# Low parts of the weights taken off GpSimd in the first mixer and behind the second, and the residual's squares summed by products alone

## The chip, the cores and the metric

The program runs on one core of one Trainium2 chip. Its time is the device time of one execution in microseconds (us). The core has five engines that work side by side and wait for each other through semaphores: TensorE (PE in the rows; PEld is its weight load) multiplies matrices, VectorE (DVE) and ScalarE (ACT) work element by element, GpSimd (POOL) does so too, and SyncE (SP) starts the transfers from memory. What a matmul gives lands in PSUM, the other tiles lie in SBUF.

## The reference

The input is one sequence of 256 tokens of width 1024, all in float32. Two blocks follow each other. The first has a hybrid mixer (a gated part and a pooled part), a SwiGLU layer, an RWKV time mix and another SwiGLU layer; the second has a mixer of convolution and attention, and then a layer with a squared ReLU. What the change touches is this:

```python
# first block, layer 0: z = rms_norm(h) @ ab_w_in, then
y_a = gmlp_spatial_gate(za[..., :512], za[..., 512:], ...)   # u * (w_s @ rms_norm(v) + b)
y_b = multiscale_pool(z[..., 1024:], pool_w, pool_scale)     # windows 2, 4, 8, 16
h = h + concat([y_a, y_b]) @ ab_w_out
# second block, behind its token mixer (whose last product is with w_out)
x = x + gate1 * rms_norm_2(y, g_post_mix)
h = rms_norm_2(x, g_pre_mlp) * (1.0 + scale2) + shift2
y = square(relu(h @ w_mlp_in)) @ w_mlp_out                   # 1024 -> 4096 -> 1024
x = x + gate2 * rms_norm_2(y, g_post_mlp)
```

## The kernel before

The residual `h` lies in SBUF with channels on the partitions: 8 tiles of 128 channels by 256 tokens. All weights stream in as 2604 blocks of 128x128, eight to a chunk of 512 KB, in the order in which the program uses them.

**Products in three parts.** Each float32 weight chunk `raw` is cut into a high part `hi` (ScalarE, line 185) and the rest `lo = raw - hi` (line 186), and each activation into `xh` and `xl`. A block's product is then three matmuls: hi with xh, hi with xl, lo with xh. `take` hands out blocks in order and has the chunks cut 16 blocks ahead. Four buffers hold `hi` and four hold `lo`, so a chunk's `hi` waits until TensorE has left the chunk four places before it.

**Who makes the low part.** `Weights.share` decides. It is added up chunk by chunk, and where the sum reaches 1 the low part goes to GpSimd instead of VectorE. It is 1 in three stretches: in the first mixer from line 686 to line 746, in the second mixer from line 1545 to line 1720, and from line 1803 in `post` to line 1854 in `mlp`. It also says where `rsqrt` and the sums of squares are worked out.

**First mixer** (`mixer`). One loop over the 8 tiles of `h` makes the pooled part and `v`. Then come the products for `u` (32 blocks, `ps<-xh,hi` and so on), and in the midst of them four products `plps` of the pooled sums `pl` with `poolw`. The sums (`s`, `pl`) and the reciprocal root for `v` (`rs_t`, `rs_y`, `rs_p`) are VectorE's. `mixps` comes next, and then the products with `ab_w_out`.

**Behind the second mixer** (`post`, then `mlp`). `post` scales the mixer's result `pu` by a factor for each token, which lies broadcast in PSUM (`bcps`), and adds it to `h`, tile by tile. `after_h` then cuts each new tile into `xh` and `xl` (scaled by the column `gs`), squares two tiles an operation on ScalarE (`sq`), and adds the squares up (`Sums`). TensorE meanwhile runs the first 6 column blocks of `w_mlp_in` on this unnormalised input (`gemm_fold`: 6 blocks for each of the 8 tiles, 48 blocks, 144 matmuls called `fold`). Inside this loop the sum over the partitions (`sums`, a product with a column of ones), the reciprocal root and its broadcast (`bcps`, `bc`) are made; when it is done, `modulate` makes the normalised `xh`, `xl` (through `mod`) for the other 26 column blocks.

**Order on an engine.** Each engine works through its own list in order. The lists are made when the program is built, by a scheduler that may move an instruction past others of its engine, so the written order is not the final one.

Of the kernel before, what the change touches and what calls it, by code (L numbers as in the profile page):

```python
# [15 lines left out]
ALU = mybir.AluOpType  # L16
AX = mybir.AxisListType

P = 128
T = 256  # L20
D = 1024
# [6 lines left out]
EPS = 1e-6  # L28
# [110 lines left out]
class Weights:  # L139


    def __init__(self, nc, dram, raw_pool, hl_pool, look=16, ahead=2):
        self.nc, self.dram, self.rp, self.hp = nc, dram, raw_pool, hl_pool
        self.order = []
        self.raw, self.hl = {}, {}
        self.nload = self.nsplit = 0
        self.look, self.ahead = look, ahead
        self.hook = None

        self.share = self.acc = 0.0  # L150

        self.whole = set()
# [78 lines left out]
class Sums:  # L231

    def __init__(self, kern, urgent=False, gp=4):
        self.k, self.urgent, self.gp = kern, urgent, gp
        self.parts = []
        self.acc = None

    def part(self):  # L240
        t = self.k.mp.tile([P, 512], F32, tag="sq" if self.parts else "acc", name="sq", bufs=2)
        self.parts.append(t)
        return t
# [4 lines left out]

    def added(self):
        n = len(self.parts)  # L250
        if n > 1 and not (n == 4 and self.urgent):

            e = self.k.nc.gpsimd if not self.k.ws.share and n <= self.gp else self.k.nc.vector
            e.tensor_tensor(out=self.parts[0], in0=self.parts[0], in1=self.parts[-1], op=ALU.add)  # L254
        if n == 4 - self.urgent:
            self.k.tt(self.parts[0][:, 0:T], self.parts[0][:, 0:T], self.parts[0][:, T:2 * T], ALU.add)

    def done(self):
        assert len(self.parts) == 4
        return self.k.token_sums([self.parts[0][:, 0:T]] + self.parts[3:4] * self.urgent)  # L260


class Kern:
# [360 lines left out]
    def mixer(self, xs, sums, nxt):  # L624
# [3 lines left out]
        st = {}  # L628
# [52 lines left out]
        for k in range(KD):  # L681
# [1 line left out]
                self.mm3(psb[m // 2][:, (m % 2) * T:(m % 2 + 1) * T], self.ws.take([win(k, 8 + m)]), X(k),  # L683
                         k == 0 and m % 2 == 0, k == KD - 1)
            self.mm3_tok(psv, self.ws.take([win(k, 4 + i) for i in range(4)]), X(k), k == 0, k == KD - 1)
        self.ws.share = 1
        for i in range(2):
            epi_v(i, psv[i])
        m = self.tiny("vm", [P, 2], tag="n2m")
# [1089 lines left out]
    def post(self, X, ks, banks, gcol, xs, xcol, sums):  # L1779


        pss = {}
        sm = Sums(self, True)

        def epi(j, ps):
            pss[j] = ps
            sm.square(ps)

        self.gemm(X, ks, banks, epi)
        r = self.rstd(sm.done(), D, EPS, 2)  # L1790
        u = self.slot("pu")
        for m in range(KD):
            self.act(u[:, m, :], pss[m // 2][:, (m % 2) * T:(m % 2 + 1) * T], AF.Copy, scale=gcol[:, m:m + 1])

        self.gg = gg = self.slot("gg", (P, 2, 512))
        for i in range(2):
            ps = self.bank("gg")
            for k in range(4):
                dg = self.mid("dg", (P, P))
                self.ts(dg, self.cst("ident", 128), self.gs[:, 24 + 4 * i + k:25 + 4 * i + k], None, ALU.mult)  # L1800
                self.mm(ps[:, k * P:(k + 1) * P], self.cst("ones", 128), dg, k == 0, k == 3)
            self.act(gg[:, i, :], ps, AF.Copy)
        self.ws.share = 1
        self.busy(BUSY_POST)
        bc = self.bcast(r, psum=True)
        self.busy(BUSY_POST)
        for j in range(4):
            for m in (2 * j, 2 * j + 1):
                t = u[:, m, :]
                self.tt(t, t, bc, ALU.mult)  # L1810
                self.tt(self.h[:, m, :], self.h[:, m, :], t, ALU.add)
            self.after_h(j, xs, xcol, sums)

    def mlp(self, xs, sums):
        nc = self.nc
        flat = lambda ap: ap.rearrange("p a t -> p (a t)")
        st = {}
# [1 line left out]
        src = lambda m: (lambda k: full("w_mlp_in_2", 0, k, m * P))  # L1819

        def stats():
            st["r"] = self.rstd(sums.done(), D, EPS)

        def bc():
            st["bc"] = self.bcast(st["r"])
# [10 lines left out]
        for m, ps in enumerate(pss):  # L1836
            nc.vector.tensor_copy(out=bias[:, m:m + 1], in_=ps[:, T:T + 1])
            r = self.mid("rf", (P, T))
# [41 lines left out]
        def mean(src, i, tt, more):  # L1880
            m = self.tiny("fm", [P, 1], tag="fm")
            self.ts(m, src[:, tt, i:i + 1], 1.0 / D, more, ALU.mult, ALU.add)
            return m
# [25 lines left out]
        m = mean(ss, 1, 0, mean(ss, 0, 0, EPS))  # L1909
        gated(0, slice(512, D), pss[0])  # L1910
        finish(0, m, (slice(0, 512), slice(512, D)))
        m = mean(ss, 0, 1, EPS)
        for i in range(2):
# [4 lines left out]
            m = mean(ss, 1 + i, 1, m)  # L1918
# [4 lines left out]
    def run(self, stop=99):  # L1923
        nc, io = self.nc, self.io
        self.h = h = self.xp.tile([P, KD, T], F32, tag="h", name="h")
        self.pvt = self.cp.tile([P, NPV], F32, tag="pv", name="pvt")
        self.cstt = self.cp.tile([P, NCST], F32, tag="cst", name="cstt")
        nc.sync.dma_start(out=self.pvt[:, 0:8], in_=io["pv"][:, 0:8])
        self.warm()

        def load_x(k):
            nc.sync.dma_start(out=h[:, k, :], in_=io["x"][:, k, :])

        load_x(0)
        for _ in self.ws.load(2):
            pass
        for k in (1, 2):
            load_x(k)
            self.ws.load_to(k)
        for k in (3, 4, 5):  # L1940
            load_x(k)
        nc.sync.dma_start(out=self.cstt[:, 0:257], in_=io["cst"][:, 0:257])

        def simple(g):

            return lambda: (self.main_x(), self.pv(g, 0, 8), [(Sums(self, gp=4 if g[:3] == "ffn" else 1), None)])

        nx = simple("mix0")()
        with self.phase(11, 6):
            xs, gcol, sums = nx  # L1950

            def split_x(k):
                self.split_scaled(xs[0][:, k, :], xs[1][:, k, :], h[:, k, :], gcol[:, k:k + 1])

            split_x(0)
            for _ in self.ws.split(2):
                pass
            for k in (1, 2):
                split_x(k)
                for _ in self.ws.split(2):  # L1960
                    pass
            split_x(3)
            self.after(1, lambda: (load_x(6), load_x(7)))
            for k in range(4, KD):
                self.after(6 * k - 22, lambda k=k: split_x(k))
            for j in range(4):
                self.after(8 * j + 12, lambda j=j: self.after_h(j, None, None, sums))
            self.after(16, lambda: nc.sync.dma_start(out=self.cstt[:, 257:], in_=io["cst"][:, 257:]))
            self.after(28, lambda: nc.sync.dma_start(out=self.pvt[:, 8:], in_=io["pv"][:, 8:]))
            nx = self.mixer(nx[0], nx[2][0][0], simple("ffn0"))  # L1970
        self.dump("h0", h)
        if stop <= 0:
            return
        ada = self.pool("ada", 1, ctx0 := ExitStack())
        self.ap = ada
        steps = self.ada_setup()
        self.ws.plan_whole(24 * NF, 1)

        self.ws.plan_whole(24 * NF + 88, 18)
        self.bg = steps[:28]  # L1980
        self.bg_rate = 28 / 520.0
        with self.phase(6, 8):
            nx = self.ffn(0, nx[0], nx[2][0][0], lambda: (None, None, [(Sums(self, True), None)]))
        self.drain_bg()
        self.dump("h1", h)
        if stop <= 1:
            ctx0.close()
            return
        ctx0.close()
        with self.phase(8, 7):  # L1990
            nx = self.rwkv(nx[2][0][0], simple("ffn1"))
        self.dump("h2", h)
        if stop <= 2:
            return
        ada = self.pool("ada2", 1, ctx0 := ExitStack())
        self.ap = ada
        steps = self.ada_setup()
        self.bg = steps[28:]
        self.bg_rate = 20 / 330.0

        def to_mixer2():
            self.drain_bg()
            self.ada_done()
            xs = self.fold_x()
            self.fold_shift(xs, self.shift1)

            nc.sync.dma_start(out=self.cst("reset", T).bitcast(I32), in_=io["pos"].partition_broadcast(P))
            return xs, self.gs[:, 0:8], [(Sums(self, gp=3), None), (Sums(self, gp=3), self.pv("fin", 0, 8))]

        with self.phase(6, 8):  # L2010
            nx = self.ffn(1, nx[0], nx[2][0][0], to_mixer2)
        self.dump("mod", self.mod)
        ctx0.close()
        self.dump("h3", h)
        if stop <= 3:
            return

        def to_mlp():
            xs = self.fold_x()
            self.fold_shift(xs, self.shift2)  # L2020
            return xs, self.gs[:, 16:24], [(Sums(self), None)]

        with self.phase(13, 4):
            ny = []
            self.mixer2(nx[0], [sm for sm, _ in nx[2]], lambda: ny.append(to_mlp()) or ny[0])
            self.dump("h4", h)
            self.mlp(ny[0][0], ny[0][2][0][0])
# [82 lines left out]
```

## Time and profile before

| | |
|---|---|
| median of 3 runs | 1151.2 us (1149.26 to 1152.41) |
| the profiled execution | 1150.61 us, of which 1148.8 us from first to last instruction |
| TensorE busy | 1098.6 us (96%) |
| VectorE, ScalarE, GpSimd busy | 852.0 us (74%), 574.9 us (50%), 188.5 us (16%) |
| granted TensorE clock, mean | 0.974 of full speed |

All times in the rows are us from the first instruction. In a row of the timeline stand the start, the duration of the merged instructions, the engine and the line of the code, the operation with what it writes and reads, their shapes and how many they are; in square brackets is how long the engine had been idle ahead of it, and what ended that. The start of the next row tells how soon the engine took up the next instruction, which can be a little ahead of the end of the one before.

### The profile page before, as it was taken

How to read it: one execution, taken by the hardware profiler on the slowest of the kernel's cores; microseconds unless marked ns; L12 is line 12 of the kernel's file. 1: busy time of each engine (PE TensorE's matmuls, PEld its weight loads, DVE VectorE, ACT ScalarE, POOL GpSimd, SP SyncE). 2: the span in 40 equal slices, each digit the busy share in tenths (PEclk: the TensorE clock that was granted, in tenths of full speed). 3: DMA queues.
4: the chain of work that ended last, by engine and by line, in shares of the span. 5: the costliest groups of instructions: out<-in, count | busy, mean ns of one | idle time of the engine just before them, and what ended most of it. 6: DMA issues, size and time to landing. Idle time of an engine off the chain costs nothing. (4 is left out here: it accounts for less than half of the span.)

```text
span 1148.8 us, 22642 instructions
## 1 busy us (share of the span) xinstructions
PE 1098.6 (96%) x9220; PEld 1032.4 (90%) x9220; DVE 852.0 (74%) x1552; ACT 574.9 (50%) x922; POOL 188.5 (16%) x137
## 2 busy tenths in 40 slices
PE   9799999999999999999999998899899997999997
PEld 7699999999887598999999998897798997999886
DVE  6878988547954846888975579799886958965444
ACT  5565444444731545654454546454545654755342
POOL 1310000002010021110000004776363014000000
PEclk9999999999998979999999999899899998999999
DMA  8468887653441310588865543444144542555552
GB/s 291 152 206 306 302 297 281 209 183 126 136 142 59 132 38 21 184 302 314 281 206 184 182 164 130 151 164 132 67 135 157 172 162 92 179 186 169 187 189 82
DMA packets 57817, 202.52 MB, mean 176 GB/s; under 512 B 6896, under 2 KB 8560, under 8 KB 57712
## 3 DMA queue, kind: packets, MB, share of 16 engines
q1 hardware_dynamic: 57712, 201.07, 51.7%
q8 instruction: 72, 1.18, 0.4%
q14 instruction: 33, 0.27, 0.1%
HBM read 199.98 MB, written 1.05 MB: 175 GB/s over the span
## 5 line engine op out<-in xcount | busy, mean ns | idle before, releaser
L185 ACT ACTIVATE hi<-raw 128x1024 fp32r<-128x1024 f32 (+1 forms) x310 | 322.5, 1048 | 265.2 <-PE ps L355 175.2
L186 DVE TENSOR_TENSOR lo<-raw,hi 128x1024 fp32r<-128x1024 f32 (+1 forms) x258 | 315.4, 1226 | 145.3 <-ACT hi L185 144.9
L355 PE MATMUL ps<-xl,hi 128*128 128x256 f32 x1104 | 313.9, 285 | 4.1 <-DVE xl L343 4.1
L355 PE MATMUL ps<-xh,hi 128*128 128x256 f32 x1104 | 316.1, 287 | 1.4 <-ACT hi L185 1.0
L355 PE MATMUL ps<-xh,lo 128*128 128x256 f32 x1104 | 311.8, 283 | 2.8 <-DVE lo L186 1.5
L355 PEld LDWEIGHTS ps<-xl,hi 128*128 128x128 f32 x1104 | 210.4, 191 | 5.4 <-DVE xl L343 5.0
L355 PEld LDWEIGHTS ps<-xh,lo 128*128 128x128 f32 x1104 | 210.3, 191 | 4.4 <-DVE lo L186 3.0
L355 PEld LDWEIGHTS ps<-xh,hi 128*128 128x128 f32 x1104 | 209.7, 190 | 3.5 <-ACT hi L185 2.3
L186 POOL TENSOR_TENSOR lo<-raw,hi 128x1024 fp32r<-128x1024 f32 x52 | 126.0, 2442 | 115.6 <-ACT hi L185 75.9
L343 DVE SCALAR_TENSOR_TENSOR cva<-up,cwh,cva 128x256 f32<-128x256 f32 x232 | 103.3, 483 | 3.2 <-ACT cva L352 1.1
L355 PE MATMUL ps<-zl,hi 128*128 128x256 f32 x352 | 99.6, 283 | 0.0
L355 PE MATMUL ps<-zh,lo 128*128 128x256 f32 x352 | 99.4, 282 | 0.0
L355 PE MATMUL ps<-zh,hi 128*128 128x256 f32 x352 | 98.7, 280 | 0.0
L254 POOL TENSOR_TENSOR sq<-sq 128x512 f32<-128x512 f32 x17 | 23.3, 1374 | 453.2 <-ACT sq L352 453.0
L343 DVE SCALAR_TENSOR_TENSOR ada<-ada,cb 128x1024 f32<-128x1024 f32 x48 | 58.6, 1222 | 16.7 <-DMA ada<-in_ada_dram 16.6
L355 PEld LDWEIGHTS ps<-zh,hi 128*128 128x128 f32 x352 | 66.9, 190 | 0.0
L355 PEld LDWEIGHTS ps<-zh,lo 128*128 128x128 f32 x352 | 66.1, 188 | 0.0
L355 PEld LDWEIGHTS ps<-zl,hi 128*128 128x128 f32 x352 | 65.8, 187 | 0.0
L355 PE MATMUL ps<-hi,zl 128*128 128x256 f32 (+1 forms) x160 | 56.1, 350 | 0.0
L355 PE MATMUL ps<-hi,zh 128*128 128x256 f32 (+1 forms) x160 | 56.0, 350 | 0.0
L355 PE MATMUL ps<-lo,zh 128*128 128x256 f32 (+1 forms) x160 | 55.9, 350 | 0.0
L352 ACT ACTIVATE s<-z 128x256 f32<-128x256 f32 x44 | 18.3, 417 | 71.2 <-DVE z L340 71.1
(438 smaller groups left out, 2260.8 us busy)
## 6 DMA issues: line engine op xcount, KB each, us to landing
raw<-in_w_dram SPq DMA_DIRECT2D x325, 512.0 KB
ada<-in_ada_dram SPq DMA_DIRECT2D x48, 512.0 KB
h<-in_x_dram SPq DMA_DIRECT2D x8, 128.0 KB
cb<-in_c_dram SPq DMA_DIRECT2D x2, 512.0 KB
out_dram<-ht SPq DMA_DIRECT2D x3, 256.0 KB
raw<-in_w_dram SPq DMA_DIRECT2D x2, 256.0 KB
cstt<-in_cst_dram SPq DMA_DIRECT2D x1, 448.5 KB
poolw<-in_poolw_dram SPq DMA_DIRECT2D x1, 256.0 KB
```

The source lines that it names most:

```text
L185: self.nc.scalar.activation(out=hi[:, s], in_=raw[:, s], func=AF.Copy)
L186: eng.tensor_tensor(out=lo[:, s], in0=raw[:, s], in1=hi[:, s].bitcast(F32), op=ALU.subtract)
L254: e.tensor_tensor(out=self.parts[0], in0=self.parts[0], in1=self.parts[-1], op=ALU.add)
L343: self.nc.vector.scalar_tensor_tensor(out=out, in0=a, scalar=s, in1=b, op0=op0, op1=op1, **k)
L352: self.nc.scalar.activation(out=out, in_=a, func=f, **k)
L355: self.nc.tensor.matmul(out=out, lhsT=lhsT, rhs=rhs, start=start, stop=stop, skip_group_check=True)
```

## The change

Two lines `self.ws.share = 1` go, so that the low parts of four chunks in the first mixer and of six chunks behind the second are made on VectorE. `Sums` gets a form `direct`: four squares are kept in one tile `sq4`, no adds are made, and `token_sums` multiplies all of them with the column of ones. It is used for the sums behind the second mixer alone. In `post` the scaling and the addition take two tiles an operation. In `mlp` the reciprocal root is asked for on VectorE by an argument, where `share` did so before.

```diff
-    def __init__(self, kern, urgent=False, gp=4):
-        self.k, self.urgent, self.gp = kern, urgent, gp
+    def __init__(self, kern, urgent=False, gp=4, direct=False):
+        self.k, self.urgent, self.gp, self.direct = kern, urgent, gp, direct
...
     def part(self):
+        if self.direct:
+            if not self.parts:
+                self.held = self.k.slot("sq4", (P, 4, 512))
+            self.parts.append(self.held[:, len(self.parts), :])
+            return self.parts[-1]
...
     def added(self):
         n = len(self.parts)
+        if self.direct:
+            return
...
     def done(self):
         assert len(self.parts) == 4
+        if self.direct:
+            return self.k.token_sums(self.parts)
...
             self.mm3_tok(psv, self.ws.take([win(k, 4 + i) for i in range(4)]), X(k), k == 0, k == KD - 1)
-        self.ws.share = 1
         for i in range(2):
             epi_v(i, psv[i])
...
-        self.ws.share = 1
         self.busy(BUSY_POST)
         bc = self.bcast(r, psum=True)
         self.busy(BUSY_POST)
         for j in range(4):
-            for m in (2 * j, 2 * j + 1):
-                t = u[:, m, :]
-                self.tt(t, t, bc, ALU.mult)
-                self.tt(self.h[:, m, :], self.h[:, m, :], t, ALU.add)
+            ms = slice(2 * j, 2 * j + 2)
+            self.tt(u[:, ms, :], u[:, ms, :], self.rb(bc), ALU.mult)
+            self.tt(self.h[:, ms, :], self.h[:, ms, :], u[:, ms, :], ALU.add)
             self.after_h(j, xs, xcol, sums)
...
-            st["r"] = self.rstd(sums.done(), D, EPS)
+            st["r"] = self.rstd(sums.done(), D, EPS, True)
...
-            return xs, self.gs[:, 16:24], [(Sums(self), None)]
+            return xs, self.gs[:, 16:24], [(Sums(self, direct=True), None)]
```

The lists of the engines show where the instructions come to stand. The first place is VectorE in the first mixer, from the last operation of the pooled sums' loop on; `zu` scales the products for `u`, and `yl` is the low part of the pooled result. Before:

```order
L340 TENSOR_TENSOR s_147<-s_147,cnt 128x16
L340 TENSOR_TENSOR zu<-ps,bc 128x512
L349 TENSOR_SCALAR rs_p<-rs_t 128x2
L343 SCALAR_TENSOR_TENSOR pl<-s_147,zb 128x256
L340 TENSOR_TENSOR rs_t<-rs_t,rs_p 128x2
L343 SCALAR_TENSOR_TENSOR rs_y<-rs_t,rs_y 128x2
L347 TENSOR_SCALAR vn<-vn,rs_y 128x512
L343 SCALAR_TENSOR_TENSOR yl<-plps,pvt,yh 128x256 x3
L186 TENSOR_TENSOR lo<-raw,hi 128x1024
```

Of the change, at the same place:

```order
L350 TENSOR_TENSOR s_147<-s_147,cnt 128x16
L186 TENSOR_TENSOR lo<-raw,hi 128x1024
L359 TENSOR_SCALAR rs_p<-rs_t 128x2
L353 SCALAR_TENSOR_TENSOR pl<-s_147,zb 128x256
L350 TENSOR_TENSOR rs_t<-rs_t,rs_p 128x2
L186 TENSOR_TENSOR lo<-raw,hi 128x1024
L353 SCALAR_TENSOR_TENSOR rs_y<-rs_t,rs_y 128x2
L350 TENSOR_TENSOR zu<-ps,bc 128x512
L357 TENSOR_SCALAR vn<-vn,rs_y 128x512
L186 TENSOR_TENSOR lo<-raw,hi 128x1024
L353 SCALAR_TENSOR_TENSOR yl<-plps,pvt,yh 128x256 x2
L186 TENSOR_TENSOR lo<-raw,hi 128x1024
```

The four low parts that were GpSimd's now stand on VectorE between the last of the pooled sums and the second half of `yl`. On TensorE three of the four `plps` products stand 19 matmuls earlier in the list than before, ahead of the first matmul that reads the first of these low parts; the fourth stays where it was.

The second place is VectorE behind the second mixer, from the first operation that reads the broadcast factor. Before:

```order
L340 TENSOR_TENSOR pu<-pu,bcps 128x256 x2
L340 TENSOR_TENSOR h<-h,pu 128x256 x2
L340 TENSOR_TENSOR pu<-pu,bcps 128x256
L343 SCALAR_TENSOR_TENSOR xl<-h,gs,xh 128x256 x2
...
L254 TENSOR_TENSOR sq<-sq 128x512
L340 TENSOR_TENSOR h<-h,pu 128x256 x2
L343 SCALAR_TENSOR_TENSOR xl<-h,gs,xh 128x256 x2
L254 TENSOR_TENSOR sq<-sq 128x512
L340 TENSOR_TENSOR sq<-sq 128x256
L349 TENSOR_SCALAR mean<-sums 128x2
```

Of the change:

```order
L350 TENSOR_TENSOR pu<-pu,bcps 128x512 x2
L350 TENSOR_TENSOR h<-h,pu 128x512 x2
L350 TENSOR_TENSOR pu<-pu,bcps 128x512
L353 SCALAR_TENSOR_TENSOR xl<-h,gs,xh 128x256 x4
L350 TENSOR_TENSOR h<-h,pu 128x512
L350 TENSOR_TENSOR pu<-pu,bcps 128x512
L186 TENSOR_TENSOR lo<-raw,hi 128x1024
L353 SCALAR_TENSOR_TENSOR xl<-h,gs,xh 128x256 x2
L350 TENSOR_TENSOR h<-h,pu 128x512
L186 TENSOR_TENSOR lo<-raw,hi 128x1024
L353 SCALAR_TENSOR_TENSOR xl<-h,gs,xh 128x256 x2
L359 TENSOR_SCALAR mean<-sums 128x2
```

The adds of the squares are gone and two low parts stand among the tiles. Of the other four, one stands ahead of this place, one inside the reciprocal root, and two right ahead of the first `mod`.

The third place is TensorE in the fold, where the products of the squares with the column of ones stand. Before there are two, behind 89 of the 144 `fold` matmuls:

```order
L355 MATMUL fold<-xh,hi 128x258
L355 MATMUL fold<-xl,hi 128x258
L355 MATMUL sums<-cstt,sq 128x1 x2
L355 MATMUL fold<-xh,lo 128x258
```

Of the change there are sixteen, behind 6, 39 and 58 `fold` matmuls (`sq_11111` is the tile `sq4`):

```order
L365 MATMUL fold<-xh,hi 128x258 x6
L365 MATMUL sums<-cstt,sq_11111 128x1 x4
L365 MATMUL fold<-xl,hi 128x258
...
L365 MATMUL sums<-cstt,sq_11111 128x1 x8
L365 MATMUL fold<-xh,hi 128x258
...
L365 MATMUL sums<-cstt,sq_11111 128x1 x4
L365 MATMUL fold<-xl,hi 128x258
```

The last of them stand 31 `fold` matmuls earlier than the two did; the broadcast `bcps` stands behind 111 in both.

## Rows read from the trace of the kernel before

**Rows 1.** Windows: stretch, its length, busy time (count) per engine, clock, DMA.
```profile
0.00:1148.00 1148.00, 1098.63 (x9220) 1032.42 (x9220) 852.05 (x1552) 574.85 (x922) 188.55 (x137) 0.97 0.52 176
...
37.95:53.77 15.82, 9.48 (x57) 8.11 (x56) 14.54 (x24) 5.58 (x9) 9.18 (x4) 0.89 0.39 134
946.12:973.71 27.59, 20.99 (x151) 20.55 (x151) 22.60 (x40) 11.68 (x20) 12.54 (x5) 0.88 0.24 78
973.71:980.00 6.29, 5.30 (x37) 4.43 (x35) 6.29 (x20) 5.12 (x10) 0.00 (x0) 1.00 0.24 81
...
946.00:955.00 9.00, 8.88 (x73) 8.83 (x73) 8.86 (x14) 4.95 (x9) 4.82 (x2) 1.00 0.17 60
```

**Rows 2.** Timeline of TensorE in the first mixer.
```profile
39.29 0.39 PE L355 MATMUL ps<-xh,lo 128*128 128x256 f32 x1 [1.06 <-POOL lo L186]
...
42.48 0.67 PE L355 MATMUL plps<-pl,poolw 128*128 128x256 f32 x2 [0.66 <-PE ps L355]
47.78 2.93 PE L355 MATMUL plps<-pl,poolw 128*128 128x256 f32 x6 [4.62 <-DVE pl L343]
...
53.77 1.95 PE L355 MATMUL mixps<-wst,vn 128*128 128x128 f32 x16
```

**Rows 3.** Timeline of GpSimd, first mixer and behind the second.
```profile
36.79 10.34 POOL L186 TENSOR_TENSOR lo<-raw,hi 128x1024 fp32r<-128x1024 f32 x4 [7.38 <-ACT hi L185]
...
951.74 2.41 POOL L186 TENSOR_TENSOR lo<-raw,hi 128x1024 fp32r<-128x1024 f32 x1 [0.17 <-ACT hi L185]
957.13 5.32 POOL L186 TENSOR_TENSOR lo<-raw,hi 128x1024 fp32r<-128x1024 f32 x2 [2.98 <-PE fold L355]
970.23 2.40 POOL L186 TENSOR_TENSOR lo<-raw,hi 128x1024 fp32r<-128x1024 f32 x1 [7.78 <-ACT hi L185]
```

**Rows 4.** Timeline of VectorE in the first mixer.
```profile
32.26 1.22 DVE L186 TENSOR_TENSOR lo<-raw,hi 128x1024 fp32r<-128x1024 f32 x1
...
36.90 2.88 DVE L340 TENSOR_TENSOR s<-s 128x512 f32<-128x512 f32 x1
39.71 2.35 DVE L349 TENSOR_SCALAR rs_y<-rs_t 128x2 int32<-128x2 int32 x1
...
44.86 2.29 DVE L343 SCALAR_TENSOR_TENSOR rs_t<-rs_t,vm 128x2 f32<-128x2 f32 x1
...
48.12 0.16 DVE L340 TENSOR_TENSOR s<-s,cnt 128x16 f32<-128x16 f32 x1
```

**Rows 5.** Timeline of VectorE behind the second mixer.
```profile
944.44 0.75 DVE L340 TENSOR_TENSOR pu<-pu,bcps 128x256 f32<-128x256 f32 x2 [1.12 <-PE bcps L355]
...
949.52 2.33 DVE L343 SCALAR_TENSOR_TENSOR xl<-h,gs,xh 128x256 fp32r<-128x256 f32 x1
951.78 2.92 DVE L254 TENSOR_TENSOR sq<-sq 128x512 f32<-128x512 f32 x1
...
956.41 0.68 DVE L254 TENSOR_TENSOR sq<-sq 128x512 f32<-128x512 f32 x1
...
958.00 4.73 DVE L343 SCALAR_TENSOR_TENSOR xl<-h,gs,xh 128x256 fp32r<-128x256 f32 x2 [0.24 <-ACT xh L352]
...
970.46 3.25 DVE L343 SCALAR_TENSOR_TENSOR mod<-h,gs,bc 128x256 f32<-128x256 f32 x3 [3.03 <-ACT bc L352]
...
974.82 1.26 DVE L343 SCALAR_TENSOR_TENSOR mod<-h,gs,bc 128x256 f32<-128x256 f32 x3
```

**Rows 6.** Timeline of TensorE behind the second mixer.
```profile
940.41 0.95 PE L355 MATMUL sums<-cstt,sq 128*128 128x1 f32 x8
...
946.12 0.98 PE L355 MATMUL fold<-xh,hi 128*128 128x258 f32 x6 [0.85 <-ACT xh L352]
...
963.94 0.98 PE L355 MATMUL sums<-cstt,sq 128*128 128x1 f32 x4 [6.27 <-DVE sq L340]
```

**Rows 7.** Timeline of ScalarE behind the second mixer.
```profile
946.38 0.62 ACT L352 ACTIVATE sq<-h 128x512 f32<-128x512 f32 x1
...
948.03 1.06 ACT L185 ACTIVATE hi<-raw 128x1024 fp32r<-128x1024 f32 x1 [0.16 <-PE fold L355]
```

## The prediction

> **What bounds the kernel now.** I read the windows first. Over the span TensorE is busy 1098.6 of 1148 us [rows 1], so a change helps only where TensorE waits or runs slowly. Then I read the two places that the change touches. In the first mixer, from 37.95 to the first `mixps` at 53.77, TensorE is busy 9.48 of 15.82 us at a granted clock of 0.89. In the fold behind the second mixer, 946.12 to 973.71, it is busy 20.99 of 27.59 us at 0.88 [rows 1]. These two stretches hold some 13 us of idle time, and their busy time is stretched by the clock.
>
> The timeline of TensorE names the waits: 1.06 us for the first low part from GpSimd, 0.66 us ahead of the first `plps`, 4.62 us for the second `pl` from VectorE [rows 2], and behind the second mixer 6.27 us for the added squares [rows 6]. The last two end on VectorE, so I read what VectorE did. In the first mixer an operation on 128x2 took 2.35 us (`rs_y`), another 2.29 us, and one on 128x512 2.88 us, beside 0.16 us for 128x16 [rows 4] and 0.68 us for another 128x512 [rows 5]. Behind the second mixer one `xl` took 2.33 us, one add of squares 2.92 us against 0.68 us later, two `xl` 4.73 us, and three `mod` 3.25 us against 1.26 us for the next three [rows 5]. The timeline of GpSimd covers these times: four low parts from 36.79 for 10.34 us, and later ones from 951.74, 957.13 (two, 5.32 us) and 970.23, each some 2.4 us long [rows 3]. The reader is to see that a small operation on VectorE is held about as long as one low part on GpSimd lasts, and that the next one runs at its usual speed. So GpSimd's low parts do not only take their own time, they stop VectorE.
>
> **Term 1, the first mixer.** Taken away from GpSimd: four low parts. Added to VectorE: four of 1.22 us [rows 4], against 2.4 us each on GpSimd.
>
> The held operations are `s` (2.88 - 0.68 = 2.20), `rs_y` (2.35 - 0.16 = 2.19) and two `rs_t` (the row at 44.86 and one like it at 42.31: 2.13 each), together 8.65 us. The first moved low part stands behind the operation that ended at 48.28 [rows 4]. Without the held time that is 39.6, so it ends at 40.9. TensorE needs it from about 38.2, since it was let go at 39.29 after 1.06 us of waiting [rows 2]. The wait grows by 1.6 us. In it now fall three of the four `plps`, which stand ahead of it. The first `plps` started at 42.48 and its `pl` stands behind two of the held operations (4.4 us), so it can start at 38.1; the other two follow by 39.5; and a product is two matmuls of 0.67 us together [rows 2]. They are done by some 40.2 and cost nothing. If that cover were gone they would cost 2.0 us.
>
> From 40.9 TensorE has 19 matmuls, the fourth `plps` and 27 matmuls. At 8.88 us for 73 [rows 1] a matmul is 0.122 us, so the sum is 2.3 + 0.7 + 3.3 = 6.3 us, and `mixps` starts at 47.2 instead of 53.77: **a gain of 6.6 us**. VectorE has to follow. From 40.9 to its second `zu`, which waits for the end of these matmuls anyhow, it has three low parts (3.7 us) and, by its list, two operations of 128x512, five of 128x256 and three small ones: with 0.68, 0.42 and 0.16 us a piece, and 0.07 us less for each that starts ahead of the end of the one before, that is some 3.2 us and ends at 47.6. So it is no more than 0.4 us late, and I count nothing for it. The transfers do not hinder either: their share in this stretch is 0.39 [rows 1]. From both sides: if all idle time and the slow clock went, the gain would be 8.0 us (6.34 idle, the rest clock); if VectorE came 2 us later, with both low parts on the path, it would be 4.6 us.
>
> **Term 2, behind the second mixer.** Two tiles an operation: three operations of 0.68 us (the 128x512 row) now stand ahead of the first `xh`, where two `pu` in 0.75 us and one `h` of about 0.4 us stood [rows 5], so the fold starts 0.8 us later, at 946.9. VectorE saves some 0.07 us an operation, 0.6 us in all; it is not waited for here.
>
> The adds are gone (three of 128x512 and one of 128x256, some 2.4 us without the held time), and with them the 6.27 us wait. In their place TensorE has 16 products with the column of ones instead of two. Four of them took 0.95 us at full clock [rows 6], 0.24 each with the pipeline's tail; I take 0.22, so 3.5 us for 16. They need the squares. ScalarE makes these right behind each pair of `xh` (0.62 us), with a `hi` of 1.06 us between [rows 7]. I work out the third square for 952.0 and the fourth for 954.8; TensorE reaches their products at 952.7 and 956.7. So no wait, with 0.7 and 1.9 us to spare.
>
> The fold then takes 144 x 0.122 = 17.5 us, plus 3.5 for the products, 0.5 for the broadcast product (two matmuls, as in the row at 42.48) and 0.2 for the first square: it ends at 946.9 + 21.7 = 968.6 instead of 973.71, **5.1 us sooner**. TensorE's clock stays at its upper level. Before, the granted clock fell behind the 6.27 us of idleness, and the fold of 27.59 us had 0.88 on the mean [rows 1].
>
> Of the six low parts on VectorE one falls into time in which it waited, two stand among the tiles, one in the root and two ahead of `mod`. Between the last `xl` and `mod` that is 3 x 1.22 = 3.7 us. The last product ends at 957.6; root, low parts, broadcast (TensorE reaches it at 964) and two more low parts put the first `mod` at 965.8 and the first normalised `xl` at 967.4, 1.2 us ahead of the fold's end. Before they were level, and TensorE lost 6.29 - 5.30 = 1.0 us behind the fold [rows 1]; I take 0.6 of that as won. The three `mod` held for 2.0 us [rows 5] help here. **Term 2: 5.7 us.** From both sides: 8.5 us, if the products hide in the weight loads and the later start is won back; 2.5 us, if the products cost what they did at the slow clock, two in 0.85 us, 0.43 each [rows 6], which is 3.4 us more.
>
> **Sum.** 6.6 + 5.7 = 12.3 us. The profiled execution took 1150.6 us and comes to 1138.3. It lies 0.6 us under the median of the runs, so the median would come to 1138.9; I say 1138.5. Outside of the two stretches TensorE is busy for 1068.1 of 1104.6 us [rows 1], so there is little waiting into which a shift could fall, and both terms should reach the end.
>
> **Rivals.**
>
> *The wait moves to the squares.* A `hi` ahead of them on ScalarE waits until TensorE has left a buffer ([rows 7]: the one at 948.03 waited for `fold`). If one of them comes 4 us later than I work out, TensorE stands at the products. For it: the spare time is only 0.7 us at the third square. Against it: the `hi` in question waits for TensorE itself, which is earlier too. Term 2 shrinks to some 2.5 us: 1141.5.
>
> *The products on TensorE are dear.* At 0.43 us each, as above, the sum is 3.4 us less: 1142. For it: the row with 0.98 us for two products. Against it: this row lies right behind the long idleness, and four took 0.95 us at full clock.
>
> *VectorE becomes the bound, and the kernel is slower.* From 946 to 955 it was busy 8.86 of 9 us [rows 1], and it gets ten low parts, 12.2 us, against 2.4 + 0.6 us taken away: 9.2 us more on an engine that TensorE waits for in both places. If none of the held time came back, that would be 1160. The held time is 8.65 us in the first mixer and 10.1 us behind the second (1.9 + 2.2 + 3.9 + 2.0 [rows 5], unheld 0.42 an `xl`), 18.8 us in all; where half of it comes back, time stays as it is. Against it: every held operation lies in a stretch in which GpSimd has a low part in hand, and from 975 on, without one, none is held [rows 3, 5]. A rule speaks for this rival. The Trainium skill, Perfetto Trace Analysis, in its section Optimizing Scalar/DVE Operations, says that with a saturated VectorE it may make sense to offload to ScalarE or even GpSimd; it adds that between VectorE and GpSimd this might not help, as they share a port into SBUF. By its first half the change goes the wrong way and the time is 1160 us; by its second half the busy time of VectorE is partly waiting, which is how I read the rows.
>
> **How the numbers follow.** My forecast gets 0.72, with a range of its own from 1134.5 to 1141.5 (both upper bounds together give 1134.1, half of both lower ones 1143). The squares get 0.12, the dear products 0.10. VectorE as the bound gets 0.06: a third of it lies within 0.3% of the time before, half of it is slower, the rest a little faster. 0.3%, or 3.5 us, is about what a measurement here can tell from no change. Range 1134 to 1144: it takes in the bounds of each term alone and the first two rivals. Faster 0.95, same 0.02, slower 0.03.
>
> **What the changed profile would show.** GpSimd has low parts in the second mixer alone. In the first mixer `rs_y` and `rs_t` take about 0.16 us, TensorE waits once for `lo` until some 40.9, and `mixps` starts near 47.2. Behind the second mixer `xl` and `mod` take some 0.4 us each, the products of the squares start without a wait, the granted clock stays near 1.0, and the fold takes some 21.7 us from its first matmul to its last, not 27.59. I am wrong if operations on 128x2 still take 2 us without GpSimd, if TensorE waits over 2 us for a square or a `lo` in the fold, or if a gain in the first mixer is lost again before the second.

## The result and the profile after

| | before | after |
|---|---|---|
| median, beside each other | 1150.24 us (1149.26 to 1152.41) | 1138.83 us (1137.48 to 1140.81) |
| ratio | | 0.9900, interval 0.9876 to 0.9924 |
| the profiled execution; its span | 1150.61; 1148.8 us | 1137.48; 1135.7 us |
| first `mixps` | 53.77 | 46.73 |
| first `pu` behind the second mixer | 944.44 | 935.25 |
| first `fold` matmul | 946.12 | 937.74 |
| first matmul behind the fold | 973.71 | 962.42 |

The kernel is 11.4 us faster. Read downwards, the lower part of the table says where in this pair of executions: 7.04 us in the first mixer, 2.15 more between it and `pu`, 0.81 lost ahead of the fold, 2.91 won in it, and 1.8 behind it (13.1 us in all). Two executions, one of the changed kernel timed again (3669.58 us) and one of the version with one tile and adds (1740.99 us), were far slower than all others and are left out of the medians below.

The windows of the kernel after, same columns as [rows 1]: the span, the first mixer, the fold, the work behind it, and four pieces of the fold.

```profile
0.00:1136.00 1136.00, 1099.32 (x9248) 1034.11 (x9248) 839.18 (x1550) 574.36 (x922) 163.57 (x127) 0.97 0.55 178
37.95:46.73 8.78, 7.88 (x56) 6.88 (x56) 8.78 (x24) 5.30 (x9) 0.00 (x0) 1.00 0.48 134
937.74:962.42 24.68, 24.68 (x179) 24.47 (x180) 16.00 (x37) 12.57 (x22) 0.00 (x0) 0.86 0.31 98
962.42:987.32 24.90, 24.88 (x207) 24.55 (x206) 24.48 (x50) 19.40 (x34) 0.00 (x0) 1.00 0.56 178
...
939.00:941.00 2.00, 2.00 (x12) 2.00 (x12) 2.00 (x5) 0.92 (x3) 0.00 (x0) 0.55 0.00 0
941.00:943.00 2.00, 2.00 (x11) 2.00 (x11) 0.19 (x2) 1.15 (x2) 0.00 (x0) 0.50 0.00 0
943.00:945.00 2.00, 2.00 (x12) 2.00 (x10) 2.00 (x4) 1.23 (x3) 0.00 (x0) 0.50 0.03 8
945.00:947.00 2.00, 2.00 (x15) 2.00 (x14) 0.56 (x1) 0.57 (x1) 0.00 (x0) 0.74 0.75 256
```

VectorE has ten more low parts (12.2 us) and is busy 12.9 us less than in [rows 1]. In the fold TensorE never waits, and yet the granted clock is 0.86 on the mean: for nearly 7 us it stood at 0.5, the lower of its two levels (1.2 GHz). For the work behind the fold, the same 207 matmuls, the window before was:

```profile
973.71:1000.43 26.72, 25.73 (x207) 24.86 (x206) 26.20 (x53) 20.35 (x35) 0.00 (x0) 1.00 0.51 169
```

The timeline of VectorE after, first mixer, against [rows 4].

```profile
36.85 0.69 DVE L350 TENSOR_TENSOR s<-s 128x512 f32<-128x512 f32 x1
37.45 0.17 DVE L359 TENSOR_SCALAR rs_y<-rs_t 128x2 int32<-128x2 int32 x1
...
38.26 0.16 DVE L353 SCALAR_TENSOR_TENSOR rs_t<-rs_t,vm 128x2 f32<-128x2 f32 x1
...
39.47 1.22 DVE L186 TENSOR_TENSOR lo<-raw,hi 128x1024 fp32r<-128x1024 f32 x1
```

What took 2.88, 2.35 and 2.29 us takes 0.69, 0.17 and 0.16. The timeline of TensorE after, first mixer, against [rows 2]:

```profile
39.05 1.13 PE L365 MATMUL plps<-pl,poolw 128*128 128x256 f32 x4 [0.34 <-DVE pl L353]
40.74 0.39 PE L365 MATMUL ps<-xh,lo 128*128 128x256 f32 x1 [0.57 <-DVE lo L186]
...
43.09 0.59 PE L365 MATMUL plps<-pl,poolw 128*128 128x256 f32 x2
...
46.73 1.95 PE L365 MATMUL mixps<-wst,vn 128*128 128x128 f32 x16
```

Where TensorE waited 1.06, 0.66 and 4.62 us, it now waits 0.34 and 0.57 us. Behind the second mixer, against [rows 6]:

```profile
937.74 0.98 PE L365 MATMUL fold<-xh,hi 128*128 128x258 f32 x6 [1.65 <-ACT xh L362]
938.66 1.39 PE L365 MATMUL sums<-cstt,sq 128*128 128x1 f32 x8
939.91 0.56 PE L365 MATMUL fold<-xl,hi 128*128 128x258 f32 x1
940.27 0.42 PE L365 MATMUL fold<-xh,lo 128*128 128x258 f32 x1
...
946.67 1.84 PE L365 MATMUL sums<-cstt,sq 128*128 128x1 f32 x16
...
950.74 0.95 PE L365 MATMUL sums<-cstt,sq 128*128 128x1 f32 x8
```

The 6.27 us wait is gone, and no product waits. New is the 1.65 us ahead of the fold, where 0.85 us stood; behind it a `fold` matmul takes 0.42 us, and 0.28 us again from 946. VectorE, against [rows 5]: four `xl` in 1.67 us (a single one took 2.33), three `mod` in 1.28 (3.25).

```profile
938.26 1.67 DVE L353 SCALAR_TENSOR_TENSOR xl<-h,gs,xh 128x256 fp32r<-128x256 f32 x4
...
960.03 1.28 DVE L353 SCALAR_TENSOR_TENSOR mod<-h,gs,bc 128x256 f32<-128x256 f32 x3
```

### The profile page after: what moved, and what is told of

Same layout as the page of the kernel before. It is cut to its first block, busy times and chain, and to the rows that moved or that the text cites. A ratio compares the mean times of both kernels' runs of the same rounds, so it can differ in the third digit from the quotient of the medians.

```text
span 1135.7 us, 22677 instructions
## 1 busy us (share of the span) xinstructions
PE 1099.3 (97%) x9248; PEld 1034.1 (91%) x9248; DVE 839.2 (74%) x1550; ACT 574.4 (51%) x922; POOL 163.6 (14%) x127
## 5 line engine op out<-in xcount | busy, mean ns | idle before, releaser
L186 DVE TENSOR_TENSOR lo<-raw,hi 128x1024 fp32r<-128x1024 f32 (+1 forms) x268 | 327.8, 1227 | 151.3 <-ACT hi L185 150.3
L186 POOL TENSOR_TENSOR lo<-raw,hi 128x1024 fp32r<-128x1024 f32 x42 | 100.9, 2415 | 86.2 <-ACT hi L185 49.6
```

The source lines that it names most:

```text
L186: eng.tensor_tensor(out=lo[:, s], in0=raw[:, s], in1=hi[:, s].bitcast(F32), op=ALU.subtract)
```

## The experiments

### One part of the change at a time

**First mixer alone**: the kernel before without its line 686.

```diff
-        self.ws.share = 1
         for i in range(2):
             epi_v(i, psv[i])
```

> The kernel before with one edit: the first mixer's four low parts go to VectorE; all behind the second mixer as before. Theory (GpSimd's low parts hold VectorE's operations): the first mixps starts at about 46.7 us instead of 53.77, rs_y and rs_t take 0.16 us each, and the whole of the 7.0 us reaches the end: 1143 us against 1150.2. Rival (the shift is lost before the second mixer, or the gain of the changed kernel comes from behind the second mixer): 1147 or more. If the further 2.2 us that the changed kernel gained between 150 and 195 us belong to the change, they appear here too, with 1141; if they differ from one execution to the next, they may or may not.

Measured: 1141.41 us against 1149.56, ratio 0.9927 (0.9912 to 0.9942): 8.1 us. Its timeline of TensorE:

```profile
41.07 0.39 PE L355 MATMUL ps<-xh,lo 128*128 128x256 f32 x1 [0.57 <-DVE lo L186]
...
47.09 1.95 PE L355 MATMUL mixps<-wst,vn 128*128 128x128 f32 x16
```

The theory holds: 6.7 us in the mixer, and they reach the end.

**Behind the second mixer, low parts alone**: adds and tiles as before.

```diff
             self.act(gg[:, i, :], ps, AF.Copy)
-        self.ws.share = 1
...
-            st["r"] = self.rstd(sums.done(), D, EPS)
+            st["r"] = self.rstd(sums.done(), D, EPS, True)
...
-            return xs, self.gs[:, 16:24], [(Sums(self), None)]
+            return xs, self.gs[:, 16:24], [(Sums(self, gp=0), None)]
```

> The kernel before with the six low parts behind the second mixer on VectorE and the root there computed as in the changed kernel; one tile an operation, and the squares are still added on VectorE, so two products instead of sixteen. Theory (the holds made the 6.27 us wait): adds of squares take 0.7 us, no xl takes 2 us; 8.0 us of held time go and three low parts of 1.22 us come ahead of the adds, so the wait of 6.27 us shrinks by about 4.3 us to some 2 us and the clock falls less: 1145 us against 1150.2. Rival (the products on TensorE are what took the wait away, since VectorE gets more work than it loses): the wait stays above 5 us, 1149 or more.

Measured: 1142.15 us, ratio 0.9932 (0.9917 to 0.9947): 7.4 us, more than the some 5 us expected. The timeline of TensorE, from the fold on:

```profile
946.22 0.98 PE L355 MATMUL fold<-xh,hi 128*128 128x258 f32 x6 [0.85 <-ACT xh L352]
959.37 0.58 PE L355 MATMUL sums<-cstt,sq 128*128 128x1 f32 x4
...
966.63 0.50 PE L355 MATMUL ps<-xh,hi 128*128 128x256 f32 x2 [1.54 <-ACT xh L352]
```

The adds are still there, and nothing waits for them: without the holds the whole 6.27 us goes, not four of it. What is left is 1.54 us behind the fold, for the first `xh` that is made from `mod`.

**Products alone**: the changed `Sums(direct=True)`, with both `share = 1` put back and one tile an operation.

```diff
+        self.ws.share = 1
         for i in range(2):
             epi_v(i, psv[i])
...
             self.act(gg[:, i, :], ps, AF.Copy)
+        self.ws.share = 1
...
-            self.tt(u[:, ms, :], u[:, ms, :], self.rb(bc), ALU.mult)
+            for m in (2 * j, 2 * j + 1):
+                self.tt(u[:, m, :], u[:, m, :], bc, ALU.mult)
```

> The kernel before with one edit behind the second mixer: the squares summed by sixteen products instead of added on VectorE. All low parts stay on GpSimd in both places, and an operation stays one tile. Theory (the holds were the loss): VectorE's adds (2.4 us) go, but xl on VectorE is still held for 2 to 4 us, so TensorE waits some 3 us for the last xl instead of 6.27 us for the adds, and the products cost TensorE 3 us: 1149 to 1151, no gain. Rival (the products are what takes the wait away): no wait of more than 1 us in the fold, a fold of 22 us instead of 27.6, 1145 against 1150.

Measured: 1144.76 us against 1149.6, ratio 0.9959 (0.9945 to 0.9973): 4.8 us. My theory missed, and the rival had the number. Its windows, fold and what follows, then VectorE:

```profile
943.71:965.21 21.50, 21.50 (x178) 21.38 (x179) 18.28 (x34) 11.20 (x19) 11.62 (x5) 1.00 0.28 83
965.21:970.00 4.79, 2.75 (x18) 2.14 (x17) 4.79 (x12) 3.49 (x7) 0.49 (x1) 1.00 0.55 182
```

```profile
952.20 2.73 DVE L353 SCALAR_TENSOR_TENSOR xl<-h,gs,xh 128x256 fp32r<-128x256 f32 x2 [0.19 <-ACT xh L362]
...
955.21 2.25 DVE L357 TENSOR_SCALAR rs_t<-mean 128x2 uint32<-128x2 uint32 x1
...
961.95 4.42 DVE L353 SCALAR_TENSOR_TENSOR mod<-h,gs,bc 128x256 f32<-128x256 f32 x3 [2.38 <-ACT bc L362]
```

VectorE is held as before, but the last `xl` ends at 954.9, before TensorE needs it: the adds had been the work that came late. The hold now costs only behind the fold, where `mod` is held and TensorE works 2.75 of 4.79 us (the granted clock stays at 1.00 there).

So either edit takes the 6.27 us wait away, and the two do not add up.

### What lets the clock fall

**One tile an operation** in the changed kernel.

```diff
-            ms = slice(2 * j, 2 * j + 2)
-            self.tt(u[:, ms, :], u[:, ms, :], self.rb(bc), ALU.mult)
-            self.tt(self.h[:, ms, :], self.h[:, ms, :], u[:, ms, :], ALU.add)
+            for m in (2 * j, 2 * j + 1):
+                t = u[:, m, :]
+                self.tt(t, t, bc, ALU.mult)
+                self.tt(self.h[:, m, :], self.h[:, m, :], t, ALU.add)
```

> The changed kernel with one tile an operation in the scaling behind the second mixer, as before. Theory (the later first xh, together with the narrow products right behind the first six fold matmuls, made the granted clock fall to 0.6 for some 5 us): the fold starts 0.8 us earlier, TensorE's wait ahead of it is 0.85 us instead of 1.65, the granted clock stays near 1.0, the fold takes some 21.5 us instead of 24.7, and the kernel takes 1135 us against 1138.8. Rival (the narrow products alone pull the clock down): the granted clock still falls behind them, the gain is 0.8 us or less, 1138 or more. Second rival (one tile an operation makes VectorE late for mod, 0.07 us an operation): 1138.8 or more with a wait behind the fold.

Measured: 1135.16 us, ratio 0.9880 (0.9860 to 0.9900). TensorE waits 0.85 us ahead of the fold again, and the clock stays in it, as the theory had it. The fold:

```profile
937.74:959.50 21.76, 21.76 (x178) 21.41 (x179) 17.28 (x43) 12.62 (x22) 0.00 (x0) 1.00 0.39 116
```

**More filler matmuls**: two tiles, and the wait filled.

```diff
-        self.busy(BUSY_POST)
+        self.busy(BUSY_POST + 14)
         for j in range(4):
```

> The changed kernel with 14 more filler matmuls (their product is used by nothing) ahead of the fold, in the time in which TensorE waits 1.65 us for the first xh. Theory (this wait is what lets the granted clock fall): the clock stays near 1.0 behind it, the fold starts at most 0.2 us later and takes some 21.7 us instead of 24.7, 1136 us against 1138.8. Rival (the narrow products alone pull the clock down): the clock falls as before, and the kernel takes 1138.8 to 1139.2.

Measured: 1136.1 us, ratio 0.9881 (0.9863 to 0.9900). The intervals of these two ratios overlap that of the changed kernel (0.9876 to 0.9924), so it is the clock in the rows that decides, not the time. The fold starts without a wait, the products still stand behind its first six matmuls, and the clock stays:

```profile
938.75:960.33 21.58, 21.58 (x178) 21.37 (x179) 15.98 (x37) 12.68 (x22) 0.00 (x0) 1.00 0.37 113
```

**Adds kept, two tiles**: `Sums(self, gp=0)` in place of `direct=True`.

> The changed kernel with the squares added on VectorE as before, and so two products instead of sixteen; two tiles an operation stays. TensorE again waits about 1.65 us for the first xh, but no product stands behind the first six fold matmuls. Theory A (the wait alone lets the granted clock fall): it falls to 0.6 to 0.7 for some 5 us as in the changed kernel, the fold takes 22 us (17.5 + 0.5 + 0.9 + 3) and the kernel 1137.5 us. Theory B (it takes the wait and the narrow products right behind it): the clock stays near 1.0, the fold takes some 19 us, and the kernel 1135 us.

Measured: 1135.48 us, ratio 0.9860 (0.9838 to 0.9882). The wait of 1.65 us without the products: the clock falls.

```profile
940.43:960.77 20.34, 20.26 (x150) 19.87 (x151) 18.13 (x40) 12.54 (x22) 0.00 (x0) 0.92 0.40 123
943.00:945.00 2.00, 2.00 (x12) 2.00 (x11) 1.87 (x5) 1.94 (x4) 0.00 (x0) 0.50 0.00 0
```

Theory A holds for the clock: here the wait does it, with or without the products; the products stay harmless where it is filled. The time does not tell the two theories apart: 1135.48 us is nearer to B's 1135 than to A's 1137.5. The fold is shorter than A had it, 20.3 us and not 22, and TensorE waits for no `mod` behind it.

**One tile and six more fillers**, for the 0.85 us that are left.

```diff
-        self.busy(BUSY_POST)
+        self.busy(BUSY_POST + 6)
```

> The changed kernel with one tile an operation and 6 more filler matmuls, which fill the 0.85 us that TensorE still waits for the first xh. Theory (a wait of 0.85 us does not let the clock fall, so filling it brings nothing): as one tile an operation alone, 1135.2, granted clock near 1.0. Rival (the clock also loses a part behind 0.85 us): 1 to 2 us less, 1133.5.

Measured: 1134.97 us, ratio 0.9861 (0.9844 to 0.9878); the fold takes 21.75 us at a clock of 1.00. Filling 0.85 us brings nothing that can be measured.

**The changed kernel again.**

> The changed kernel once more, timed beside the next two on one chip, since the gains over it (3 to 5 us) are near what a measurement can tell. Theory (the fall of the granted clock belongs to this kernel's wait of 1.65 us, in every execution): 1138.8, the granted clock falls to about 0.6 in the fold again, and the fold takes some 24.7 us. Rival (the fall was an accident of the one profiled execution): clock near 1.0, fold 21.7 us, 1136.

Measured: 1138.3 us, ratio 0.9893 (0.9876 to 0.9910). The clock falls again, for a shorter time:

```profile
939.99:963.15 23.16, 23.16 (x178) 22.96 (x179) 15.99 (x37) 12.56 (x22) 0.00 (x0) 0.93 0.31 105
943.00:945.00 2.00, 2.00 (x11) 2.00 (x11) 0.38 (x1) 0.95 (x1) 0.00 (x0) 0.51 0.00 0
```

The fold's length is thus not one number for one kernel: 24.68 us and 23.16.

### The low parts' move alone

**One tile an operation and the adds kept**, timed twice: the changed kernel with the diffs of the last two kinds together.

> The changed kernel without its two other edits: one tile an operation and the squares added on VectorE, so that only the low parts and the root's form differ from the kernel before. Theory (the holds were the whole loss; the products replace a wait that is gone without them, at 3.5 us on TensorE less what VectorE's adds cost behind the fold): 1149.6 less the 8.1 us of the first mixer alone and the 7.4 us behind the second alone is 1134 us; TensorE waits about 1.5 us for the first mod behind the fold. Rival (the products relieve VectorE, and with both places changed its adds are missed): 1137 or more.

> The version with one tile an operation and the squares added on VectorE, beside the changed kernel on one chip. Theory: 1134.3, 4.5 us below the changed kernel, with the clock near 1.0 in the fold. Rival (the earlier difference came from the chip or its day): within 2 us of the changed kernel.

Measured: 1134.34 us, ratio 0.9859 (0.9841 to 0.9876), and 1134.1, ratio 0.9854 (0.9835 to 0.9873), here beside the changed kernel's 1138.3. It has the lowest median, 4.2 us ahead of the changed kernel, with less code. Its lead over two tiles with adds (1135.48), one tile with products (1135.16) and the same with fillers (1134.97) is about 1 us, less than can be measured. The windows over the fold and the wait behind it, and over what follows, and the first matmuls behind that wait:

```profile
937.81:958.20 20.39, 18.85 (x150) 18.12 (x150) 19.53 (x51) 12.55 (x21) 0.00 (x0) 1.00 0.43 131
958.20:968.20 10.00, 9.85 (x76) 9.39 (x77) 9.67 (x22) 7.45 (x15) 0.00 (x0) 1.00 0.24 79
```

```profile
958.20 0.50 PE L365 MATMUL ps<-xh,hi 128*128 128x256 f32 x2 [1.53 <-ACT xh L362]
```

TensorE is busy 2.9 us less than with one tile and products (18.85 against 21.76), but waits 1.53 us for `xh` behind `mod`, which the products had covered.

This wait is nearly as long as the 1.65 us ahead of the fold, and no fall of the clock follows it: 1.00 over the next 10 us. The other two profiles with such a wait (1.54 us, the repetition and the low parts alone) show the same. So the runs show that the wait ahead of the fold brings the fall in its place; they do not show that the length of a wait decides.

### What holds VectorE

**GpSimd reads**: in the changed kernel's first mixer GpSimd subtracts the same tiles once more.

```diff
             eng.tensor_tensor(out=lo[:, s], in0=raw[:, s], in1=hi[:, s].bitcast(F32), op=ALU.subtract)
+            if self.extra is not None:
+                self.nc.gpsimd.tensor_tensor(out=self.extra, in0=raw, in1=hi.bitcast(F32), op=ALU.subtract)
```

> The changed kernel with four extra subtractions on GpSimd in the first mixer, of the same raw and hi into a tile that nobody reads; the low parts that TensorE uses stay on VectorE. Theory (GpSimd's operation holds VectorE's ones that read two operands from SBUF): rs_y and rs_t take 2.2 us again, low parts on VectorE too some 3.5 us, and the first mixps is back at 54 to 57 us, 1146 to 1149 in all, though no matmul waits for GpSimd. Rival (VectorE's operations were held by something that went with the low parts, as their semaphores or a late buffer): rs_y and rs_t stay at 0.16 us, the first mixps at 47 us, 1139.

Measured (one run): 1144.89 us, a little under the 1146 to 1149 expected. GpSimd, VectorE and TensorE:

```profile
37.01 10.28 POOL L189 TENSOR_TENSOR extra<-raw,hi 128x1024 fp32r<-128x1024 f32 x4 [7.38 <-ACT hi L186]
```

```profile
37.12 2.88 DVE L353 TENSOR_TENSOR s<-s 128x512 f32<-128x512 f32 x1
39.92 2.30 DVE L362 TENSOR_SCALAR rs_y<-rs_t 128x2 int32<-128x2 int32 x1
42.13 0.41 DVE L356 SCALAR_TENSOR_TENSOR pl<-s,zb 128x256 f32<-128x256 f32 x1
42.47 2.30 DVE L353 TENSOR_TENSOR rs_t<-rs_y 128x2 f32<-128x2 f32 x1
```

```profile
56.22 1.95 PE L368 MATMUL mixps<-wst,vn 128*128 128x128 f32 x16
```

Nothing waits for GpSimd's result here, and the holds of [rows 4] are back to within 0.05 us; the first `mixps` comes 9.5 us later. The low parts on VectorE start behind GpSimd's last subtraction and keep 1.21 us, other than I expected.

**GpSimd only writes**: a fill in place of the subtraction.

```diff
+                self.nc.gpsimd.tensor_copy(out=self.extra[:, 0:1], in_=hi[:, n - 1:n])
+                self.nc.gpsimd.memset(self.extra.bitcast(F32), 0.0)
```

> The changed kernel with four fills of a 128x1024 tile by GpSimd in the first mixer, each behind a copy of one column of hi (which sets its time); the tile is read by nobody. The Trainium skill, SBUF - State Buffer, section Who interferes with whom, has it that a VectorE operation with two inputs in SBUF contends with a GpSimd operation that reads SBUF, not with one that only writes it. By that rule rs_y and rs_t stay at 0.16 us, a low part at 1.2 us, the first mixps at 46.7 us, 1139 in all. Rival (any GpSimd operation on a large tile holds VectorE): operations of 2 us appear on VectorE next to the fills, and the first mixps comes some us later.

Measured (one run): 1140.36 us, the first `mixps` at 47.22. GpSimd and VectorE:

```profile
37.28 0.96 POOL L190 MEMSET extra<- 128x1024 f32 x1
...
38.57 0.95 POOL L190 MEMSET extra<- 128x1024 f32 x1
...
39.97 0.95 POOL L190 MEMSET extra<- 128x1024 f32 x1
```

```profile
37.77 0.49 DVE L363 TENSOR_SCALAR rs_y<-rs_t 128x2 int32<-128x2 int32 x1
...
39.02 0.42 DVE L357 SCALAR_TENSOR_TENSOR pl<-s,zb 128x256 f32<-128x256 f32 x1
...
39.93 1.21 DVE L187 TENSOR_TENSOR lo<-raw,hi 128x1024 fp32r<-128x1024 f32 x1
```

`pl` and the low part, with two inputs each, keep their 0.42 and 1.21 us while a fill is on. `rs_y`, with one input, does not: it ends at 38.26, with the first fill (38.24). The first half is the rule of the Trainium skill, SBUF - State Buffer, section Who interferes with whom, and this trace agrees. My 0.16 us for `rs_y` was wrong; the same section lists `tensor_scalar` among the operations that can enter a mode which contends with GpSimd, where their operands allow it, and the 0.49 us would fit that. That is argued, not shown: the trace does not name modes, and it has this one case. A fill lasts 0.95 us, so the operations of 2 us that the rival asked for could not have come of one.

## Why the prediction was right, and where it was not

The prediction said 1138.5 us; it is 1138.8, and 1138.3 when timed again. By its steps:

- **Term 1, 6.6 us: right.** The first moved low part ended at 40.7 (40.9 was worked out), `mixps` came at 46.73 (47.2), a gain of 7.0 us. The three `plps` cost nothing in the wait, and VectorE was not late. The first mixer alone is worth 8.1 us at the end.
- **The holds: right, and shown** by the extra subtraction. The held time was put at 18.8 us. VectorE's busy time would have grown by 9.2 us by the prediction's own count and fell by 12.9, so 22 us of it had been waiting. With one tile and the adds kept, where the low parts' move is all that differs from the kernel before, it is 841.75 us: 10.3 less, with 12.2 us of work added.
- **Both terms should reach the end: right on the whole.** The 2.15 us won between the first mixer and `pu` in this pair belong to no edit that I can name. The changed kernel profiled again had its first `pu` at 937.51, 6.9 us earlier than before and not 9.2; and the products-alone kernel, whose first mixer is the old one (first `mixps` 54.30), started its fold 2.4 us earlier than before. One profile differs from the next by so much.
- **Term 2, 5.7 us: the step that failed is "TensorE's clock stays at its upper level".** The later start was right (0.8 us), and so was the fold of 21.7 us, wherever the clock did stay: 21.76, 21.58 and 21.75 us in three variants. In the changed kernel the wait that two tiles an operation bring grew to 1.65 us, the clock fell behind it, and the fold took 24.68 and 23.16 us: 3.0 and 1.5 us more. I had costed the 0.8 us as a delay only. Behind the fold 1.8 us were won, not 0.6 (24.90 us against 26.72 for the same 207 matmuls): no `mod` is held, and TensorE's 1.0 us of waiting is gone; the rest has no cause that the runs show. Together 3.9 us in the first profile, and 5.4 in the second by the same count (-0.8 + 4.4 + 1.8).
- **The sum: near in part by luck.** With the same two tiles, and the clock kept up by fillers, the kernel took 1136.1 us, 2.4 us under the forecast. What the fall of the clock cost (1.5 to 3.0 us) is about what the first mixer (8.1 us at the end, not 6.6) and the work behind the fold (1.8 us, not 0.6) gave beyond their terms.
- **Two bounds are miscounted**, without bearing on the forecast: the dear products leave 5.7 - 3.4 = 2.3 us of term 2, not 2.5, and 1143 is near what both lower bounds give together (1150.6 - 4.6 - 2.5 = 1143.5), not half of them.
- **"The adds are gone, and with them the 6.27 us wait": only half the reason.** With the adds kept the wait goes too, and with the low parts left on GpSimd it goes as well.
- **The rivals.** The squares came in time. The products cost 0.21 us each at full clock ((21.76 - 18.85) / 14), where 0.22 was taken. VectorE is not the bound. The half of the rule quoted there that speaks for offloading to GpSimd does not fit this kernel: the offload cost it 8.1 and 7.4 us in its two places. The other half, that between these two engines it might not help, fits.

What stays open: how long the lower clock lasts (nearly 7 us in the profile of the changed kernel, some 3.4 us in those of its repetition and of the one with adds), why no fall follows the wait of 1.5 us behind the fold, and why the stretch from the first `mixps` to the first `pu` differs by up to 4.8 us between the profiles (887.7 us with the products alone, 892.5 us with the fills).

## What to carry to other kernels

Where a tiny operation on VectorE takes as long as an operation on GpSimd that lies beside it, count GpSimd's time as VectorE's: moving that work onto the "busier" engine freed more of it than it cost. When two edits aim at the same wait, run each alone, since either may be enough and the second then only adds its price. Where a change makes TensorE wait longer ahead of a long run of matmuls, cost that run at the lower clock as well, look at the granted clock behind the wait, and fill the gap or make the operations that it waits for smaller.

## What was unexpected of the hardware

- In all five profiles with 1.65 us of waiting ahead of the fold the granted clock fell to 0.5 between 1 and 2 us after the fold's start; in all nine with 0.85 us or less it stayed at 1.00 there. It also stayed behind a single wait of 1.53 or 1.54 us at the end of the fold, in three profiles.
- A 128x2 operation with one input ended only with a plain fill on GpSimd (0.49 us instead of 0.17, one case), while two-input operations beside fills were not held.
- Beside back-to-back subtractions on GpSimd one operation of VectorE waits for each, and twice the next one slips through at its usual 0.41 us.
